# Transposing the larger softmax blocks of seven attention heads by DMA, as half words

## The chip, the cores and the metric

The kernel runs on one core of one Trainium2 chip. The metric is the device time of one execution in microseconds; the time before is the median of three runs. The engines are named as the profile names them: PE is TensorE (PEld its weight loads), DVE is VectorE, ACT is ScalarE, POOL is GpSimd, SP is SyncE, whose queue issues most DMAs.

## The reference

One sequence of 1024 tokens, model width 1024, float32. A recurrent layer (RG-LRU, width 1280), then one attention layer of 8 heads (MLA: keys and values from a 256-wide latent, queries from a 384-wide one, 64 rope dimensions shared by the heads of the key), then a norm. The part that matters here:

```
def one_block(args):                      # one of 8 blocks of 128 queries
    s = einsum("bqhd,bkhd->bhqk", qn_b, k_nope) + einsum("bqhr,bkr->bhqk", qr_b, k_rope)
    s = where(kpos <= qpos, s * ATTN_SCALE, -inf)
    p = softmax(s, axis=-1)
    return einsum("bhqk,bkhd->bqhd", p, v)
...
y = o.reshape(bsz, seq, 8 * 128) * silu(gate)
x = rms_norm(x + y @ w_out, final_norm)
```

## The kernel before, in words

Everything is kept transposed, features on the 128 partitions and tokens along the free axis. Each float32 operand of a product is held as two float32r tiles, a high part and the rest (`hl`: ACT copies the high part, DVE subtracts), and a product is three matmuls: high by high, high by low, low by high (`mm3`). A "page" is a tile of 128 x 1024 words from a pool of 36.

The recurrent layer, the projections of the attention layer and the spills of gates (`gd`), query ropes (`qsd`) and the latent (`kvd`) to HBM take the first 500 us or so. Then comes attention:

- `items` lists 64 items, 8 heads (`hd`) by 8 query blocks (`qb`) of 128 queries. Block `qb` sees `qb + 1` key blocks of 128.
- `scores(hd, qb, ...)` runs two items ahead (`LOOK`). It makes a block of scores in PSUM (tile `s`, two buffers), queries on partitions; DVE adds the mask and takes the maximum, ACT takes the exponential with its sum, DVE the reciprocal and the scaling (L869). The result `p_` is a page.
- `transposes(qb, p_, pts)` turns it, 128 x 128 at a time, on TensorE into PSUM (L877; tile `pm`, four buffers), and `hl` splits the result into the tiles `pt`, high and low, where keys are on partitions.
- `pv(hd, g, pts)` multiplies the values by four query blocks at once (`g` is 0 for blocks 0 to 3, 1 for 4 to 7), one item after the last of them (`PVD`), multiplies by the gate (a page, loaded per head) and splits the result `y`. The split `y` of heads 0 to 5 (`NSPILL`) is spilled to `ysd` by DMAs on POOL's queue.
- `kq` makes the next head's keys and queries and `vals` the values of a pair of heads; their pieces are spread over the items by hand (`KQ_AT`, `V_AT`, `V0_AT`). In the last head `dpart` does part of the output product, from `y` that `yload` has brought back by SP's queue, and `wout` loads the output weights.

The output product, the residual and the norm follow in three chunks of tokens.

The order on each engine is made when the program is built, from priorities in the order of the text and the scheduler's own idea of what is ready; weight loads (`wload`) have their priority raised by 100 instructions (`WPRI`). An engine then runs its instructions in that order, each waiting for its semaphores. DMAs of one queue are issued in order too.

Of the kernel before, what the change touches and what calls it, by code (L numbers as in the profile page):

```python
# [8 lines left out]

F32 = mybir.dt.float32  # L10
F32R = mybir.dt.float32r
AF = mybir.ActivationFunctionType
ALU = mybir.AluOpType
AX = mybir.AxisListType
# [3 lines left out]
S = 1024  # L18
# [3 lines left out]
NH = 8  # L22
# [1 line left out]
SCALE = 192 ** -0.5  # L24
NEG = -1e30
P = 128
NPAGES = 36
NSPILL = 6
WPRI = 100
WOUT_AT = (-1, 1, 2)  # L30
# [13 lines left out]
SPN = (5, 0)  # L44
# [13 lines left out]
def trunk(tc, xT, wina, vecs, wgate, wouta, winc, wuk, wuv, wuq, wuqr, woutb, rope, outT):  # L58
# [15 lines left out]

    def page(dt=F32R):
        return pgs.tile([P, S], dt, tag="pg", name=nm("pg"))

    def f(ap):
        return ap.bitcast(F32)

    def hl(src, hi, lo):
        A.activation(out=hi, in_=src, func=AF.Copy)  # L82
        V.tensor_tensor(out=lo, in0=src, in1=f(hi), op=ALU.subtract)  # L83
# [39 lines left out]
    def hs(h):  # L123
        return slice(h * HW, (h + 1) * HW)
# [44 lines left out]


    pr_ = ExitStack()
    rbp = pr_.enter_context(tc.tile_pool(name="rbp", bufs=1))
    pa = ExitStack()
    ta = pa.enter_context(tc.tile_pool(name="ta", bufs=2))
# [81 lines left out]
    def xsplit(k, c=slice(0, S)):  # L256
        g = vec[:, NA + k:NA + k + 1]
        if len(xs) == k:
            xs.append((page(), page()))
        xh, xl = xs[k][0][:, c], xs[k][1][:, c]  # L260
        A.activation(out=xh, in_=xrs[k][:, c], func=AF.Copy, scale=g)
        V.scalar_tensor_tensor(out=xl, in0=xrs[k][:, c], scalar=g, in1=f(xh), op0=ALU.mult, op1=ALU.subtract)  # L262
# [195 lines left out]

    def fput(i, j, src):
        if fx[i][j // 2] is None:  # L460
            fx[i][j // 2] = (page(), page())
        hi, lo = fx[i][j // 2]
        hl(src, hi[:, hs(j % 2)], lo[:, hs(j % 2)])

# [358 lines left out]
    def vals(pair, half):  # L823

        if half == 0:
            vt[pair] = []
        uh, ul = wload(wuv[pair], 512)
        t = (page(), page())
        vt[pair].append(t)

        def piece(sp):
            ps = pm()
            for sb in range(2):
                o = ps[:, sb * 256:(sb + 1) * 256]
                c0 = (half * 4 + sp * 2 + sb) * P
                for kt in range(2):
                    ch, cl = ckv[kt][0][:, c0:c0 + P], ckv[kt][1][:, c0:c0 + P]
                    u = slice(kt * 256, (kt + 1) * 256)
                    T.matmul(out=o, lhsT=ch, rhs=uh[:, u], start=kt == 0, stop=False)
                    T.matmul(out=o, lhsT=ch, rhs=ul[:, u], start=False, stop=False)  # L840
                    T.matmul(out=o, lhsT=cl, rhs=uh[:, u], start=False, stop=kt == 1)
            hl(ps, t[0][:, hs(sp)], t[1][:, hs(sp)])

        return [lambda sp=sp: piece(sp) for sp in range(2)]

    def scores(hd, qb, k, q, qs):
        nk = (qb + 1) * P
        ps = pss.tile([P, S], F32, tag="s", name=nm("s"))
        ql = slice(qb * P, nk)

        o = P if nk == 5 * P else 0
        sc = ps[:, o:o + nk]
        for c0, c1 in ((0, min(nk, HW - o)), (HW - o, nk)):
            if c0 >= c1:
                continue
            c = slice(c0, c1)
            T.matmul(out=sc[:, c], lhsT=q[0][:, ql], rhs=k[0][:, c], start=True, stop=False)  # L857
            T.matmul(out=sc[:, c], lhsT=q[0][:, ql], rhs=k[1][:, c], start=False, stop=False)  # L858
            T.matmul(out=sc[:, c], lhsT=q[1][:, ql], rhs=k[0][:, c], start=False, stop=False)  # L859
            T.matmul(out=sc[:, c], lhsT=qs[:, ql], rhs=R1[:, c], start=False, stop=False)  # L860
            T.matmul(out=sc[:, c], lhsT=qs[:, ql], rhs=R2[:, c], start=False, stop=True)  # L861
        V.tensor_tensor(out=sc[:, ql], in0=sc[:, ql], in1=mask, op=ALU.add)
        m = tp.tile([P, 1], F32, tag="m", bufs=4, name=nm("m"))
        V.tensor_reduce(out=m, in_=sc, axis=AX.X, op=ALU.max, negate=True)  # L864
        p_ = page(F32)
        l = tp.tile([P, 1], F32, tag="l", bufs=4, name=nm("l"))
        A.activation(out=p_[:, 0:nk], in_=sc, func=AF.Exp, bias=m, accum_out=l)  # L867
        V.reciprocal(out=l, in_=l)
        V.tensor_scalar(out=p_[:, 0:nk], in0=p_[:, 0:nk], scalar1=l, scalar2=None, op0=ALU.mult)  # L869
        return p_  # L870

    def transposes(qb, p_, pts):
        for b0 in range(0, qb + 1, 4):
            b1 = min(qb + 1, b0 + 4)
            ps = pm()
            for b in range(b0, b1):
                T.transpose(out=ps[:, (b - b0) * P:(b - b0 + 1) * P], in_=p_[:, b * P:(b + 1) * P], identity=ident)  # L877
            th, tl = pts[b0 // 4]
            c = (qb % 4) * P
            src = ps[:, 0:(b1 - b0) * P].rearrange("p (k q) -> p k q", q=P)  # L880
            hl(src, th[:, 0:b1 - b0, c:c + P], tl[:, 0:b1 - b0, c:c + P])

    def pv(hd, g, pts):
        ps = pm()
        v = vt[hd // 2]
        nb = 4 * (g + 1)
        for b in range(nb):
            c = slice(max(0, b - 4 * g) * P, HW)
            vs = slice((b % 4) * 256 + (hd % 2) * P, (b % 4) * 256 + (hd % 2) * P + P)
            vh, vl = v[b // 4][0][:, vs], v[b // 4][1][:, vs]  # L890
            th, tl = pts[b // 4][0][:, b % 4, c], pts[b // 4][1][:, b % 4, c]
            T.matmul(out=ps[:, c], lhsT=vh, rhs=th, start=b == 0, stop=False)  # L892
            T.matmul(out=ps[:, c], lhsT=vh, rhs=tl, start=False, stop=False)  # L893
            T.matmul(out=ps[:, c], lhsT=vl, rhs=th, start=False, stop=b == nb - 1)  # L894
        y = gates[hd][:, hs(g)]
        V.tensor_tensor(out=y, in0=ps, in1=y, op=ALU.mult)
# [7 lines left out]
    gates = []  # L904
    ysb = [None] * NH

    ysd = dp.tile([NSPILL, 2, P, S], F32, name="ysd")
# [27 lines left out]
    heads[0], kqwork = kq(0)  # L935
    for wk in kqwork:
        wk()
    kqwork = []
    vwork = vals(0, 0) + vals(0, 1)
    dwork = []  # L940
    ny = 0
    items = [(hd, qb) for hd in range(NH) for qb in range(8)]
    pend = {}
    pts = {}
    late = []
    for i in range(LOOK):
        pend[items[i]] = scores(*items[i], *heads[0])
    for i, (hd, qb) in enumerate(items):
        if qb == 0:
            gt = page(F32)  # L950
            nc.sync.dma_start(out=gt, in_=gd[hd])
            gates.append(gt)
            if hd + 1 < NH:
                heads[hd + 1], kqwork = kq(hd + 1)
        if qb == VQB and hd // 2 + 1 < NH // 2:
            vwork += vals(hd // 2 + 1, hd % 2)
# [6 lines left out]
        if i == 8 * (NH - 1) + DSTART:  # L963
            dwork = [lambda a=a: dpart(*a) for a in DPART]
        for wl, n in ((kqwork, KQ_AT[qb]), (vwork, V0_AT[qb] if hd == 0 and qb < 4 else V_AT[qb]), (dwork, D_AT[qb - DSTART] if i >= 8 * (NH - 1) + DSTART else 0)):
            for _ in range(min(n, len(wl))):
                wl.pop(0)()
        g = qb // 4
        if qb % 4 == 0:
            pts[hd, g] = [tuple(tp.tile([P, 4, HW], F32R, tag=f"pt{i}", name=nm("pt")) for i in range(2)) for _ in range(g + 1)]  # L970
# [3 lines left out]
        if qb % 4 == 3:  # L974
            late.append((i, hd, g, pts.pop((hd, g))))
        j = i - 8 * (NH - 1)
# [137 lines left out]
```

## Time and profile before

| | us |
|---|---|
| median of 3 runs | 875.47 (875.17 to 876.12) |
| the profiled execution, whole | 876.11 |
| its span, first to last instruction | 874.3 |
| busy PE / DVE / ACT / POOL | 857.5 / 659.4 / 517.0 / 75.1 |
| one head of attention (heads 1 to 6) | 31.0 |
| mean granted TensorE clock | 0.994 |

Busy time is the time in which an engine has an instruction in work; matmuls overlap, so the pitch from start to start says what one costs. "A <- B" in the waits means that A's engine sat idle until B ended. In groups of instructions the columns are line, engine, operation, tiles and shapes, count, busy us, mean ns of one, and the idle time before them.

### The profile page before, as it was taken

To read this page: it belongs to the slowest core of one execution; us is meant where nothing else is said; L and a number is where in the kernel's file an instruction comes from. 1 tells how busy PE (TensorE), PEld (TensorE's weight loads), DVE (VectorE), ACT (ScalarE), POOL (GpSimd) and SP (SyncE) were. 2 spreads that over 40 slices of the span, in tenths; PEclk is the share of its full clock that TensorE was granted. 3 is DMA by queue.
4 is the path that set the end of the run, shared out by engine and by line. 5 is a ranking of instruction groups with operands and counts; after the bars stand their busy time and mean duration, and the time that the engine had idled before them with its cause. 6 is when DMAs were issued, how large, how long until landed. Compare 5 with 4: busy or idle time off the path is not lost.

```text
span 874.3 us, 12183 instructions
## 1 busy us (share of the span) xinstructions
PE 857.5 (98%) x4326; PEld 729.6 (83%) x4326; DVE 659.4 (75%) x1224; ACT 517.0 (59%) x956; POOL 75.1 (9%) x145
## 2 busy tenths in 40 slices
PE   8999999999999999999999999999999999999995
PEld 7788888888887888888778888988998998888995
DVE  7798778777877764779988956887797887775453
ACT  7457787777687542699885645555565554431222
POOL 1010110011000100000212320000000000010000
PEclk9999999999999999999999999999999999999998
DMA  8333333333212545133535664222231326666031
GB/s 289 99 97 97 97 96 97 109 101 92 79 37 81 179 132 175 49 108 111 177 122 205 216 229 119 76 82 97 70 112 67 111 67 258 214 216 204 27 126 66
DMA packets 51789, 109.00 MB, mean 125 GB/s; under 512 B 6544, under 2 KB 16656, under 8 KB 51728
## 3 DMA queue, kind: packets, MB, share of 16 engines
q1 hardware_dynamic: 36240, 67.45, 24.2%
q0 software_dynamic: 15216, 40.51, 13.9%
q8 instruction: 34, 0.56, 0.3%
q10 hardware_dynamic: 272, 0.26, 0.1%
q14 instruction: 27, 0.22, 0.1%
HBM read 81.46 MB, written 26.21 MB: 123 GB/s over the span
## 4 chain that ended last, share of the span: by engine, by line
PE 62%; issue 21%; DVE 7%; ACT 4%; DMA 2%; POOL 2%; SPq 0%; DVEq 0%; POOLq 0%; ACTq 0%
PE ps L115 7%; PE ps L116 7%; PE ps L114 7%; PE pm L116 6%; PE pm L115 6%; PE pm L114 6%; PE pm L877 4%; PE pm L894 2%; PE pm L893 2%; PE s L858 2%; PE s L859 2%; PE s L857 2%; PE s L861 2%; PE s L860 2%; PE pm L892 2%
## 5 line engine op out<-in xcount | busy, mean ns | idle before, releaser
L114 PE MATMUL ps<-pg,wh 128*128 128x512 f32 x672 | 262.4, 392 | 3.4 <-DVE tk L627 1.2
L115 PE MATMUL ps<-pg,wh 128*128 128x512 f32 x672 | 262.4, 390 | 0.3 <-DVE pg L262 0.3
L116 PE MATMUL ps<-pg,wl 128*128 128x512 f32 x672 | 262.2, 390 | 0.1
L114 PEld LDWEIGHTS ps<-pg,wh 128*128 128x128 f32 x672 | 126.4, 188 | 31.9 <-DVE tk L627 1.6
L115 PEld LDWEIGHTS ps<-pg,wh 128*128 128x128 f32 x672 | 126.5, 188 | 27.7 <-DVE pg L262 0.6
L116 PEld LDWEIGHTS ps<-pg,wl 128*128 128x128 f32 x672 | 126.6, 188 | 27.1 <-DVE wl L83 1.0
L82 ACT ACTIVATE pt<-pm 128x512 fp32r<-128x512 f32 (+2 forms) x96 | 44.4, 490 | 59.0 <-PE pm L877 55.8
L867 ACT ACTIVATE pg<-s,m 128x128 f32<-128x128 f32 (+3 forms) x64 | 47.5, 743 | 48.0 <-DVE m L864 43.3
L114 PE MATMUL pm<-pg,pg 128*128 128x256 f32 (+1 forms) x192 | 61.9, 322 | 0.0
L115 PE MATMUL pm<-pg,pg 128*128 128x256 f32 (+1 forms) x192 | 61.6, 321 | 0.0
L116 PE MATMUL pm<-pg,pg 128*128 128x256 f32 (+1 forms) x192 | 61.3, 319 | 0.0
L83 DVE TENSOR_TENSOR pt<-pm,pt 128x512 fp32r<-128x512 f32 (+2 forms) x96 | 50.6, 547 | 2.2 <-ACT pt L82 2.1
L864 DVE TENSOR_REDUCE m<-s 128x1 f32<-128x128 f32 (+3 forms) x64 | 48.1, 753 | 1.0
L83 DVE TENSOR_TENSOR wl<-wr,wh 128x512 fp32r<-128x512 f32 (+2 forms) x57 | 32.8, 578 | 17.2 <-ACT wh L82 17.1
L358 DVE SCALAR_TENSOR_TENSOR t<-xb,vec,t 128x512 f32<-128x512 f32 x60 | 44.8, 746 | 0.4
L82 ACT ACTIVATE wh<-wr 128x512 fp32r<-128x512 f32 (+2 forms) x57 | 30.8, 543 | 23.8 <-PE ps L115 9.7
L82 ACT ACTIVATE pg<-pg 128x512 fp32r<-128x512 f32 x42 | 26.2, 630 | 29.9 <-DVE pg L412 18.3
L877 PE MATMUL pm<-ident,pg 128*128 128x128 f32 x288 | 42.3, 274 | 0.3 <-DVE pg L869 0.3
L116 PE MATMUL pm<-pg,wl 128*128 128x512 f32 x108 | 42.3, 392 | 0.0
L115 PE MATMUL pm<-pg,wh 128*128 128x512 f32 x108 | 42.3, 392 | 0.0
L114 PE MATMUL pm<-pg,wh 128*128 128x512 f32 x108 | 42.1, 390 | 0.0
L857 PE MATMUL s<-pg,pg 128*128 128x512 f32 (+2 forms) x96 | 37.2, 388 | 2.0 <-ACT pg L867 2.0
(223 smaller groups left out, 1789.6 us busy)
## 6 DMA issues: line engine op xcount, KB each, us to landing
wr<-wina SPq DMA_DIRECT2D x40, 256.0 KB, 2.8
wh<-wina POOLq DMA_DIRECT2D x36, 256.0 KB, 2.9
wa<-winc SPq DMA_DIRECT2D x24, 256.0 KB, 2.7
ysd<-pg POOLq DMA_DIRECT2D x12, 512.0 KB, 3.2
pg<-ysd SPq DMA_DIRECT2D x12, 512.0 KB, 8.3
wr<-wouta SPq DMA_DIRECT2D x16, 256.0 KB, 2.7
t<-xT SPq DMA_DIRECT2D x16, 256.0 KB, 4.0
x1d<-t POOLq DMA_DIRECT2D x16, 256.0 KB, 3.4
```

Of the source, the lines that this page charges most:

```text
L82: A.activation(out=hi, in_=src, func=AF.Copy)
L83: V.tensor_tensor(out=lo, in0=src, in1=f(hi), op=ALU.subtract)
L114: T.matmul(out=ps, lhsT=w[0], rhs=r[0], start=first, stop=False, skip_group_check=more)
L115: T.matmul(out=ps, lhsT=w[0], rhs=r[1], start=False, stop=False, skip_group_check=more)
L116: T.matmul(out=ps, lhsT=w[1], rhs=r[0], start=False, stop=last, skip_group_check=more)
L358: V.scalar_tensor_tensor(out=xc, in0=xb[:, j:j + HW], scalar=cwv[j], in1=xc, op0=ALU.mult, op1=ALU.add)
L857: T.matmul(out=sc[:, c], lhsT=q[0][:, ql], rhs=k[0][:, c], start=True, stop=False)
L858: T.matmul(out=sc[:, c], lhsT=q[0][:, ql], rhs=k[1][:, c], start=False, stop=False)
L859: T.matmul(out=sc[:, c], lhsT=q[1][:, ql], rhs=k[0][:, c], start=False, stop=False)
L864: V.tensor_reduce(out=m, in_=sc, axis=AX.X, op=ALU.max, negate=True)
L867: A.activation(out=p_[:, 0:nk], in_=sc, func=AF.Exp, bias=m, accum_out=l)
L877: T.transpose(out=ps[:, (b - b0) * P:(b - b0 + 1) * P], in_=p_[:, b * P:(b + 1) * P], identity=ident)
```

## The change

In heads 0 to 6, blocks 5, 6 and 7 (`QD = 5`) are no longer transposed by TensorE. `scores` gives GpSimd a copy of the scaled block as 16-bit halves, all first halves of the words in front and all second halves behind; SP issues one DMA transpose of these 128 x 128 blocks of half words from SBUF to SBUF, back into the page of `p_`; GpSimd joins the halves to words in the copy's page. The split (`psplit`) then reads SBUF instead of PSUM. Such a block is split three items after its turn (`HLAG = 3`), so that blocks 5 to 7 of a head are split at items 0 to 2 of the next, and `pv` of its second half comes at item 3.

With it: the scaling moves from DVE to ACT; the tiles `pt` become one tile for each half and part, without the columns that the causal mask never uses, one buffer each; gates are loaded by halves into a pool of their own; `y` of heads 0 to 5 is spilled unsplit, and `yload` reads it twice, on SP and with a cast on POOL, and DVE subtracts; the pieces of `kq` go to blocks 4 to 6, those of `vals` to even heads; the page pool has 32 pages, and four more are in a pool that ends before attention.

```
-NPAGES = 36
+NPAGES = 32
+NX = 4
-KQ_AT = (1, 0, 1, 0, 2, 0, 0, 0)
-V0_AT = (1, 1, 2, 0)
-V_AT = (0, 0, 0, 0, 0, 0, 1, 1)
+KQB = 2
+KQ_AT = (0, 0, 0, 0, 1, 1, 2, 0)
+V_AT = (0, 0, 1, 1, 0, 1, 1, 0)
+VQB = (1, 4)
+G_AT = (1, 5)
-VQB = 4
+QD = 5
+HLAG = 3
+ROW = 384
...
     (scores)
-        V.tensor_scalar(out=p_[:, 0:nk], in0=p_[:, 0:nk], scalar1=l, scalar2=None, op0=ALU.mult)
-        return p_
+        A.activation(out=p_[:, 0:nk], in_=p_[:, 0:nk], func=AF.Copy, scale=l)
+        if qb < QD or hd == NH - 1:
+            return p_
+        c = pgs.tile([P, 2 * S], U16, tag="pg", name=nm("pu"))
+        p16 = p_.bitcast(U16)
+        G.tensor_copy(out=c[:, 0:2 * nk].rearrange("p (t n) -> p t n", t=2),
+                      in_=p16[:, 0:2 * nk].rearrange("p (n t) -> p t n", t=2))
+        nc.sync.dma_start_transpose(out=p16[:, 0:2 * nk].rearrange("p (b q) -> p b q", q=P), in_=c[:, 0:2 * nk])
+        G.tensor_copy(out=c[:, 0:2 * nk].rearrange("p (n t) -> p t n", t=2),
+                      in_=p16[:, 0:2 * nk].rearrange("p (t n) -> p t n", t=2))
+        return c
...
+    def psplit(qb, c, pt):
+        for b0 in range(0, qb + 1, 4):
+            b1 = min(qb + 1, b0 + 4)
+            bysplit(c.bitcast(F32)[:, b0 * P:b1 * P], qb, b0, b1, pt)
...
     (pv)
-        y = gates[hd][:, hs(g)]
+        y = gates[hd][g]
         V.tensor_tensor(out=y, in0=ps, in1=y, op=ALU.mult)
-        if g == 0:
-            ysb[hd] = (page(), page())
-        hl(y, ysb[hd][0][:, hs(g)], ysb[hd][1][:, hs(g)])
-        if hd < NSPILL and g == 1:
-            for i in range(2):
-                DQ.dma_start(out=ysd[hd, i], in_=f(ysb[hd][i]))
+        if hd < NSPILL:
+            DQ.dma_start(out=ysd[hd, :, hs(g)], in_=y)
+        else:
+            if g == 0:
+                ysb[hd] = (page(), page())
+            hl(y, ysb[hd][0][:, hs(g)], ysb[hd][1][:, hs(g)])
...
     def yload(hd):
-        ysb[hd] = (page(), page())
-        for i in range(2):
-            nc.sync.dma_start(out=f(ysb[hd][i]), in_=ysd[hd, i])
+        hi, lo = ysb[hd] = (page(), page())
+        nc.sync.dma_start(out=f(lo), in_=ysd[hd])
+        G.dma_start(out=hi, in_=ysd[hd])
+        V.tensor_tensor(out=lo, in0=f(lo), in1=f(hi), op=ALU.subtract)
...
+    def block(i, hd, qb):
+        g = qb // 4
+        if qb % 4 == 0:
+            n = (4 * HW if g else 0) + 4 * ROW + P
+            pts[hd, g] = tuple(tp.tile([P, n], F32R, tag=f"pt{g}{a}", bufs=1, name=nm("pt")) for a in range(2))
+        (psplit if qb >= QD and hd < NH - 1 else transposes)(qb, pend.pop((hd, qb)), pts[hd, g])
+        if qb % 4 == 3:
+            late.append((i, hd, g, pts.pop((hd, g))))
...
     for i, (hd, qb) in enumerate(items):
+        if qb == KQB and hd + 1 < NH:
+            heads[hd + 1], kqwork = kq(hd + 1)
+        if hd % 2 == 0 and qb in VQB:
+            vwork += vals(hd // 2, VQB.index(qb))
+        if qb in G_AT:
+            gt = tp.tile([P, HW], F32, tag="gt", bufs=3, name=nm("gt"))
...
         if late and i - late[0][0] >= PVD:
             pv(*late.pop(0)[1:])
-        transposes(qb, pend.pop((hd, qb)), pts[hd, g])
+        while wait and wait[0][0] <= i:
+            block(i, *wait.pop(0)[1:])
+        if qb >= QD and hd < NH - 1:
+            wait.append((i + HLAG, hd, qb))
+        else:
+            block(i, hd, qb)
```

More of the change, by code (lines that the diff above doesn't have):

```diff
@@ L11 @@
 F32R = mybir.dt.float32r
+U16 = mybir.dt.uint16
 AF = mybir.ActivationFunctionType
@@ L258, in xsplit @@
         if len(xs) == k:
-            xs.append((page(), page()))
+            xs.append((page(), page()) if k >= NX // 2 else (xpage(), xpage()))
         xh, xl = xs[k][0][:, c], xs[k][1][:, c]
@@ L868, in scores, with rows, bysplit, transposes @@
         V.reciprocal(out=l, in_=l)
-        V.tensor_scalar(out=p_[:, 0:nk], in0=p_[:, 0:nk], scalar1=l, scalar2=None, op0=ALU.mult)
-        return p_
-    def transposes(qb, p_, pts):
+        A.activation(out=p_[:, 0:nk], in_=p_[:, 0:nk], func=AF.Copy, scale=l)
[9 more added lines that the diff above has]
+        return c
+    def rows(t, qb, b0, b1):
+        o, w, c, b = 0, ROW, (qb % 4) * P, b0
+        if qb >= 4:
+            if b0 < 4:
+                w = HW
+            else:
+                o, b = 4 * HW, b0 - 4
+        d = P if w == ROW and c == ROW else 0
+        return t[:, o + d:o + d + 4 * w].rearrange("p (b s) -> p b s", s=w)[:, b:b + b1 - b0, c - d:c - d + P]
+    def bysplit(src, qb, b0, b1, pt):
+        src = src[:, 0:(b1 - b0) * P].rearrange("p (b q) -> p b q", q=P)
+        hl(src, *(rows(t, qb, b0, b1) for t in pt))
+    def transposes(qb, p_, pt):
         for b0 in range(0, qb + 1, 4):
@@ L937, in trunk @@
         wk()
-    kqwork = []
-    vwork = vals(0, 0) + vals(0, 1)
-    dwork = []
+    kqwork, vwork, dwork = [], [], []
     ny = 0
     items = [(hd, qb) for hd in range(NH) for qb in range(8)]
-    pend = {}
-    pts = {}
+    pend, pts, gates = {}, {}, {}
     late = []
@@ L947, in trunk @@
         pend[items[i]] = scores(*items[i], *heads[0])
-    for i, (hd, qb) in enumerate(items):
[L949 to L956, printed above, removed]
+    def block(i, hd, qb):
[6 more added lines that the diff above has]
+            late.append((i, hd, g, pts.pop((hd, g))))
+    wait = []
+    for i, (hd, qb) in enumerate(items):
+        j = i - 8 * (NH - 1)
+        if qb == KQB and hd + 1 < NH:
[4 more added lines that the diff above has]
+            gt = tp.tile([P, HW], F32, tag="gt", bufs=3, name=nm("gt"))
+            g = G_AT.index(qb)
+            nc.sync.dma_start(out=gt, in_=gd[hd, :, hs(g)])
+            gates.setdefault(hd, []).append(gt)
         if i + LOOK < len(items):
```

32 lines of the change are left out of this document (14 added, 18 removed).

## The prediction

> **What bounds the kernel now.** I read first the busy times and the waits, then the attention stage alone, then the chain in it. Attention (a loop over 64 items, 8 heads by 8 query blocks) runs from about 528 to 784 us.
>
> ```profile
> span 874.3 us, 12183 instructions
> PE 857.5 (98%) x4326; PEld 729.6 (83%) x4326; DVE 659.4 (75%) x1224; ACT 517.0 (59%) x956; POOL 75.1 (9%) x145
> PE s L857 <- ACT pg L867: 2.0, 2, 1.1
> ```
>
> TensorE is busy nearly all the time; its longest wait for anybody totals 2.0 us. The stretches, one per head (columns: span, then busy us and count of PE, PEld, DVE, ACT, POOL, then clock, DMA share, GB/s), say the same of this stage:
>
> ```profile
> 584.60:615.60 31.00, 31.00 (x188) 27.80 (x187) 25.58 (x58) 17.33 (x39) 1.06 (x2) 1.00 0.28 88
> 739.60:784.00 44.40, 43.19 (x243) 36.92 (x242) 34.97 (x73) 17.88 (x41) 3.71 (x7) 1.00 0.67 232
> ```
>
> A head takes 31.0 us and TensorE is busy for 31.0 of them. Whatever leaves its queue comes off the time, and whatever it waits for is added. The chain inside one head shows what the transposes cost it (start, us on the chain):
>
> ```profile
> 553.59 0.57 PE pm L877 x5
> 556.45 0.65 PE pm L877 x6
> 559.10 0.76 PE pm L877 x7
> 561.91 0.87 PE pm L877 x8
> ```
>
> **Transposes removed.** Blocks 5, 6 and 7 of seven heads leave TensorE: 0.65 + 0.76 + 0.87 = 2.28 us a head, 16.0 us in all. Nothing is added to TensorE: the value products read the same columns from another layout, so this term is all gain as long as TensorE never waits.
>
> **The new chain.** Where TensorE used to transpose two items after the scores, a block now goes: scores, softmax, GpSimd copy (halves apart), DMA transpose on SP, GpSimd copy (joined), split by ACT and DVE, then `pv`. The cover is the TensorE work queued between the scores of block 7 and the `pv` that needs it. Its matmuls start at this pitch:
>
> ```profile
> 640.66 0.39 PE L861 MATMUL s<-pg,qs 128*128 128x512 f32 x1
> 640.89 0.34 PE L857 MATMUL s<-pg,pg 128*128 128x384 f32 x1
> 641.07 0.35 PE L858 MATMUL s<-pg,pg 128*128 128x384 f32 x1
> 650.10 0.28 PE L859 MATMUL s<-pg,pg 128*128 128x128 f32 x1
> 650.21 0.27 PE L860 MATMUL s<-pg,qs 128*128 128x128 f32 x1
> 651.08 0.28 PE L841 MATMUL pm<-wh,pg 128*128 128x256 f32 x1
> 651.20 0.29 PE L839 MATMUL pm<-wh,pg 128*128 128x256 f32 x1
> ```
>
> So 0.23 us for 512 columns, 0.18 for 384, 0.11 and 0.12 for 128 and 256. Between lie: a query half (9 x 0.23 = 2.1), both key halves (12 x 0.23 = 2.8), the next head's scores 0 to 5 (0.6, 0.6, 0.9, 1.15, 1.5, 1.75: 6.4 unrounded), the six small transposes of its blocks 0 to 2 (at 0.87/8 = 0.11 each, 0.7), and two pieces of values (2 x 12 x 0.12 = 2.9; two before the head change, or two after it): 14.9 us, the same for even and odd heads.
>
> Against it stands the chain. One softmax of 1024 columns with nothing beside it shows in the last head:
>
> ```profile
> 742.45 0.31 DVE s L862
> 742.78 1.24 DVE m L864
> 744.04 1.21 ACT pg L867 x2
> 745.28 0.16 DVE l L868
> 745.63 0.67 DVE pg L869
> 746.44 1.06 PE pm L877 x8
> ```
>
> That is 3.9 us from 742.45 to 746.3. The scaling moves from DVE to ACT, where 1024 columns SBUF to SBUF take 1139 ns; the split of a first half costs 632 ns there and about as much on DVE:
>
> ```profile
> L261 ACT ACTIVATE pg<-pg,vec 128x1024 fp32r<-128x1024 f32 x7 | 8.0, 1139 | 0.6 <-DMA pg<-xT 0.6
> L83 DVE TENSOR_TENSOR pg<-pg,pg 128x512 fp32r<-128x512 f32 x12 | 8.2, 682 | 0.0
> L82 ACT ACTIVATE pg<-pg 128x512 fp32r<-128x512 f32 x12 | 7.6, 632 | 1.9 <-DVE pg L896 1.5
> ```
>
> Softmax 4.4 us, split 1.3 us: 5.7, to which two copies and a transpose come.
>
> GpSimd copies 2048 half words for block 7 (1536 and 1792 for blocks 5 and 6). No row has such a copy. The nearest:
>
> ```profile
> L1058 POOL TENSOR_TENSOR pg<-pg,acc 128x256 f32<-128x256 f32 x2 | 1.8, 898 | 88.9 <-DVE acc L151 88.9
> masks.py:199 POOL TENSOR_SCALAR_AFFINE_SELECT ident<-ident 128x128 f32<-128x128 f32 x1 | 0.3, 325 | 0.0
> masks.py:197 POOL MEMSET ident<- 128x128 f32 x1 | 0.2, 204 | 0.3 <-POOLq L1106 0.3
> L1106 POOL MEMSET const-float32-0.0<- 128x1 f32 x1 | 0.1, 98 | 0.2 <-issue 0.2
> ```
>
> With 0.1 us fixed, an element costs 0.83 ns written only, 1.77 ns read and written, 3.1 ns with two inputs. A copy reads once and writes once, so it lies between the first two; I take 1.5 ns, 3.2 us for block 7 (bounds 1.8 and 6.5).
>
> The transpose moves 512 KB. The nearest rows move as much or less in plain copies, issued on SP, and the price of an issue there:
>
> ```profile
> pg<-gd SPq DMA_DIRECT2D x8, 512.0 KB, 4.0
> wr<-wuv SPq DMA_DIRECT2D x8, 256.0 KB, 2.7
> pg<-ysd SPq DMA_DIRECT2D x12, 512.0 KB, 8.3
> 554.36 0.33 SPq L91 DMA_DIRECT2D wr<-wuq  x1
> ```
>
> I take 4.0 us, the single load of that size, not the 8.3 of twelve issued in a heap; below, 2.7. [...] No run so far shows a transpose.
>
> Chain: 5.7 + 3.2 + 4.0 + 3.2 = 16.1 us against 14.9: late by 1.2 us, seven times 8.4 us. How much of it TensorE idles depends on its order, which is not the order of the text:
>
> ```profile
> 765.50 0.33 PE L893 MATMUL pm<-pt,pg 128*128 128x384 f32 x1
> 765.67 0.39 PE L114 MATMUL pm<-pg,pg 128*128 128x512 f32 x1
> 765.90 0.34 PE L894 MATMUL pm<-pt,pg 128*128 128x384 f32 x1
> ```
>
> In the last head an output product stands between two matmuls of `pv`: the scheduler fills by readiness. The next scores (2.0 us) and query half (2.1) are there to fill with. I count half of the lateness, 4.2 us.
>
> **Edits costed at nothing.** The scaling on ACT costs 1.0 ns a column, some 5.5 us a head, less two y splits of 0.63: 17.33 + 4.3 = 21.6 of 28.7 us, hidden; DVE gets about 4 us a head lighter by it, and 1.4 by the y splits. The spill of y is halved; the reload's high half goes through GpSimd's queue, and six subtractions of 1024 columns (2 x 0.68 each, 8.2 us) fall on DVE in the last head, which has 44.4 - 35.0 = 9.4 us free and 4 more from the scaling; were that cover gone, up to 8 us. GpSimd gets per head 10,752 elements (16 us at 1.5 ns) and two spill issues: 17 of 28.7 us; the spills queue behind copies, but nothing reads them before the last head. SP's queue stalls behind each transpose's wait for its copy. Queued there: gate halves (needed three and six items later) and weights, which are issued early by priority; the value weights of an even head at block 4 are the tight ones (2.7 + 1.3 us), nothing if the priority puts them ahead of the transposes, 4 x 4.0 us if not. The moves of `kq` and `vals`, the smaller page pool, and half gates change no count of TensorE's work.
>
> **Sum.** The profiled execution took 876.1 us (span 874.3), 0.6 over the median of 875.47. 876.1 - 16.0 + 4.2 = 864.3; against the median, 863.7. I say 864. With all lateness refilled 859.5, with none 868.
>
> **Rivals.**
>
> *DVE comes too late for the splits* (18 in 100). From block 7 to block 2 of the next head TensorE has only 5 to 6 us of work, and DVE nearly 9: four masks (1.2), maxima (2.2 by columns from the 1.24), reciprocals (0.6), the six splits (3.6) and the small ones (1.0). And where DVE and GpSimd both worked on SBUF, at the kernel's end, both had two inputs there:
>
> ```profile
> 866.77 0.43 DVE L151 SCALAR_TENSOR_TENSOR acc<-t,t 128x256 f32<-128x256 f32 x1
> 867.23 3.16 DVE L1058 TENSOR_TENSOR pg<-pg,acc 128x256 f32<-128x256 f32 x6
> 867.34 1.76 POOL L1058 TENSOR_TENSOR pg<-pg,acc 128x256 f32<-128x256 f32 x2 [88.86 <-DVE acc L151]
> ```
>
> Six at 0.43 make 2.6 us, they took 3.16: 0.3 us lost per GpSimd instruction of 0.9 us, some 1 us per copy if it grows with the length. The new splits read two inputs from SBUF, where the old ones read one from PSUM. Against it: the splits are wanted only at `pv`, two or three items on. If it leaves 2.0 us of idle a head in all, 14 us instead of 4.2: 873.5, still faster; from 2.28 us a head on, nothing is gained. [...]
>
> *The transpose is issued in pieces and the change is slower* (17 in 100). If SP issues one piece per 128 x 128 half words, block 7 has 16, at 0.33 us each 5.3 us, and the last lands 2.7 us later: 8.0 us instead of 4.0. The chain is then 20.1 us, late by 5.2, seven times 36 us: 877.7 with half refilled, 896 with none; 887 between. It decides from a transpose of 5.1 us (nothing refilled) to 7.4 us (half). For it speaks that no row shows this instruction; against it that plain copies of the size are one issue.
>
> [...]
>
> *GpSimd becomes the bound* (7 in 100). At the two-input rate of 3.1 ns a head's copies take 33.3 us, with two spill issues 34.4 us against 31: 24 us slower, 899. It decides at 2.8 ns. For it speaks only the row with two inputs.
>
> **How the numbers follow.** My forecast, 859.5 to 868, has 52 in 100; 2 more lie below it (a wait of the last head gone). I call the time the same within 0.2%, 873.7 to 877.2, about what a measurement of this kernel can tell. Faster: 54 and 8 of the DVE rival's 18, 62. Same: 7 of that rival and 1 of the pieces, 8. Slower: 3 of the DVE rival, 16 of the pieces, the small pieces and GpSimd, 30. The range 859 to 890 holds the forecast, the DVE rival and more than half of the pieces; the forecast's own range is 859.5 to 868.
>
> **What would show it.** TensorE has 141 of 288 transposes left. Right: a head of 28.7 to 30 us, with TensorE busy in nearly all of it, its waits at `pv` for DVE's split below 1 us a head; GpSimd copies near 3.2 us and the DMA landing near 4 us for block 7; ACT near 21.6 us a head. Wrong: waits of 2.3 us and more a head ahead of `pv` or of the scores (for ACT's exp, if softmax queues behind the splits); copies well over 3.2 us; a landing over 5 us; DVE instructions with two SBUF inputs well over 0.68 us.

## The result, and the profile after

The change makes the kernel slower: 923.77 us median of 4 runs (922.84 to 925.99) against 875.8 us before on the same chip, ratio 1.0551, 95% interval 1.0527 to 1.0574. The forecast was 864.

The page of the changed kernel, in the order read before: span, busy times, granted clock in tenths over 40 slices, the chain that ended last, and TensorE's three longest waits (us in total, times, longest).

```profile
span 920.9 us, 11981 instructions
PE 869.1 (94%) x4179; PEld 731.2 (79%) x4179; DVE 645.1 (70%) x1154; ACT 553.7 (60%) x1008; POOL 159.4 (17%) x193
...
PEclk9999999999999999999999998998989979799998
...
PE 45%; issue 19%; DMA 12%; ACT 8%; DVE 8%; POOL 8%; SPq 0%; POOLq 0%; DVEq 0%; ACTq 0%
...
PE s L869 <- ACT pg L88: 18.3, 7, 3.7
PE s L869 <- ACT pg L879: 10.7, 9, 2.9
PE s L870 <- DVE pg L89: 3.4, 5, 1.7
```

TensorE has its 147 matmuls fewer, 4179 against 4326. Its idle time went from 874.3 - 857.5 = 16.8 to 920.9 - 869.1 = 51.8 us, 35.0 more; its busy time rose by 11.6 us although 16 us of transposes had gone. So there are two losses: idle, and matmuls that take longer. The idle is not at `pv` (no such row), where the prediction looked for it. It is at `scores`, in the first items of each head: seven times for the split of the next head's keys (L88 of ACT, one for each of seven head changes), nine times for the exponential that frees a score bank, one of the two buffers of the tile `s` (L879).

The stage in windows (as before: span, busy and count by engine, clock, DMA share, GB/s):

```profile
590.00:610.00 20.00, 15.20 (x81) 13.07 (x80) 13.85 (x31) 13.94 (x31) 6.52 (x3) 0.83 0.52 114
610.00:630.00 20.00, 20.00 (x109) 17.48 (x108) 10.58 (x20) 10.26 (x19) 6.09 (x5) 1.00 0.45 93
630.00:650.00 20.00, 15.98 (x75) 13.56 (x75) 14.12 (x32) 13.42 (x32) 6.49 (x3) 0.83 0.41 98
```

The long blocks in the middle of a head (610 to 630) run as they should. Both losses sit at the head changes: TensorE busy for 15.2 of 20 us, at a mean clock of 0.83. From the second head on, heads began every 31.0 us before; now the steps are 33.9 to 39.7 us.

One head change, from 626 us on, engine by engine (start, us, engine, line, operation, and in brackets the idle time before it and what ended it): ACT first, then GpSimd, VectorE and TensorE.

```profile
628.67 1.15 ACT L881 ACTIVATE pg<-pg,l 128x1024 f32<-128x1024 f32 x1
630.12 0.60 ACT L88 ACTIVATE pg<-pm 128x512 fp32r<-128x512 f32 x1
633.24 0.63 ACT L88 ACTIVATE pt<-pu 128x512 fp32r<-128x512 f32 x1 [2.52 <-POOL pu L891]
633.78 0.58 ACT L88 ACTIVATE pg<-pm 128x512 fp32r<-128x512 f32 x1
...
631.04 2.17 POOL L891 COPY pu<-pg 128x1792 uint16<-128x1792 uint16 x1 [5.29 <-DMA pg<-pu]
633.12 1.90 POOL L888 COPY pu<-pg 128x2048 uint16<-128x2048 uint16 x1
639.45 2.52 POOL L891 COPY pu<-pg 128x2048 uint16<-128x2048 uint16 x1 [4.44 <-DMA pg<-pu]
...
633.90 1.66 DVE L89 TENSOR_TENSOR pt<-pu,pt 128x512 fp32r<-128x512 f32 x1 [2.46 <-ACT pt L88]
...
634.41 0.47 PE L869 MATMUL s<-pg,pg 128*128 128x128 f32 x1 [3.72 <-ACT pg L88]
634.68 0.52 PE L853 MATMUL pm<-wh,pg 128*128 128x256 f32 x1
635.00 0.41 PE L851 MATMUL pm<-wh,pg 128*128 128x256 f32 x1
```

ACT stands still for 2.52 us for block 6's joined words (633.24), and the key split that TensorE needs stands right behind it (633.78). TensorE waits 3.72 us for that, and then its matmuls of 256 columns start every 0.21 us, not every 0.12. GpSimd, in order too, holds block 7's first copy back until block 6 is joined: scaled at 629.82 (628.67 + 1.15), copied from 633.12. And VectorE's split of block 6, with both operands in SBUF, takes 1.66 us beside a GpSimd copy, not 0.69.

### The profile page after: what moved, and what is told of

Its sections match the earlier page's. It is cut to its first block, busy times and chain, and to the rows that moved or that the text cites. A ratio compares the mean times of both kernels' runs of the same rounds, so it can differ in the third digit from the quotient of the medians.

```text
span 920.9 us, 11981 instructions
## 1 busy us (share of the span) xinstructions
PE 869.1 (94%) x4179; PEld 731.2 (79%) x4179; DVE 645.1 (70%) x1154; ACT 553.7 (60%) x1008; POOL 159.4 (17%) x193
## 3 DMA queue, kind: packets, MB, share of 16 engines
q1 hardware_dynamic: 74832, 73.94, 28.3%
## 4 chain that ended last, share of the span: by engine, by line
PE 45%; issue 19%; DMA 12%; ACT 8%; DVE 8%; POOL 8%; SPq 0%; POOLq 0%; DVEq 0%; ACTq 0%
PE ps L122 10%; PE ps L121 10%; PE ps L120 9%; DMA pg<-pu 9%; PE pm L121 4%; PE pm L122 4%; PE pm L120 4%; POOL pu L888 4%; POOL pu L891 3%; ACT wa L519 2%; ACT wh L88 1%; DVE wl L89 1%; DVE pg L89 1%; POOL wh L103 1%; DVE t L421 1%
## 5 line engine op out<-in xcount | busy, mean ns | idle before, releaser
L120 PE MATMUL ps<-pg,wh 128*128 128x512 f32 x568 | 220.6, 390 | 2.2 <-DVE tk L639 1.3
L121 PE MATMUL ps<-pg,wh 128*128 128x512 f32 x568 | 221.1, 389 | 0.1
L122 PE MATMUL ps<-pg,wl 128*128 128x512 f32 x568 | 221.0, 389 | 0.1
L120 PEld LDWEIGHTS ps<-pg,wh 128*128 128x128 f32 x568 | 106.4, 188 | 25.6 <-DVE tk L639 1.7
L121 PEld LDWEIGHTS ps<-pg,wh 128*128 128x128 f32 x568 | 106.6, 188 | 22.7 <-DVE pg L89 0.5
L122 PEld LDWEIGHTS ps<-pg,wl 128*128 128x128 f32 x568 | 106.6, 188 | 22.6 <-DVE wl L89 0.6
L879 ACT ACTIVATE pg<-s,m 128x128 f32<-128x128 f32 (+3 forms) x64 | 47.2, 738 | 39.0 <-DVE m L876 30.0
L869 PE MATMUL s<-pg,pg 128*128 128x512 f32 (+2 forms) x96 | 40.7, 429 | 29.1 <-ACT pg L88 18.3
L891 POOL COPY pu<-pg 128x1536 uint16<-128x1536 uint16 (+2 forms) x21 | 46.8, 2228 | 77.5 <-DMA pg<-pu 77.4
L881 ACT ACTIVATE pg<-pg,l 128x128 f32<-128x128 f32 (+3 forms) x64 | 48.9, 773 | 17.8 <-DVE l L880 17.8
L89 DVE TENSOR_TENSOR pt<-pu,pt 128x512 fp32r<-128x512 f32 (+2 forms) x42 | 34.9, 832 | 29.3 <-ACT pt L88 28.6
L888 POOL COPY pu<-pg 128x1536 uint16<-128x1536 uint16 (+2 forms) x21 | 35.3, 1681 | 93.1 <-ACT pg L881 93.1
L103 POOL DMA_DIRECT2D wh<-wina x36 | 19.2, 533 | 181.3 <-PE ps L122 169.3
L869 PEld LDWEIGHTS s<-pg,pg 128*128 128x128 f32 x96 | 20.4, 215 | 37.8 <-ACT pg L88 20.3
L89 DVE TENSOR_TENSOR wl<-wr,wh 128x512 fp32r<-128x512 f32 (+2 forms) x57 | 33.7, 594 | 18.6 <-ACT wh L88 18.5
L88 ACT ACTIVATE pt<-pu 128x512 fp32r<-128x512 f32 (+2 forms) x42 | 23.5, 571 | 34.7 <-POOL pu L891 34.7
L88 ACT ACTIVATE wh<-wr 128x512 fp32r<-128x512 f32 (+2 forms) x57 | 30.5, 539 | 21.1 <-PE ps L121 11.5
```

The source lines that it names most:

```text
L120: T.matmul(out=ps, lhsT=w[0], rhs=r[0], start=first, stop=False, skip_group_check=more)
L121: T.matmul(out=ps, lhsT=w[0], rhs=r[1], start=False, stop=False, skip_group_check=more)
L122: T.matmul(out=ps, lhsT=w[1], rhs=r[0], start=False, stop=last, skip_group_check=more)
L881: A.activation(out=p_[:, 0:nk], in_=p_[:, 0:nk], func=AF.Copy, scale=l)
L888: G.tensor_copy(out=c[:, 0:2 * nk].rearrange("p (t n) -> p t n", t=2), in_=p16[:, 0:2 * nk].rearrange("p (n t) -> p t n", t=2))
L891: G.tensor_copy(out=c[:, 0:2 * nk].rearrange("p (n t) -> p t n", t=2), in_=p16[:, 0:2 * nk].rearrange("p (t n) -> p t n", t=2))
```

## The experiments

Each change is shown against the changed kernel unless it says otherwise; times are medians. The ratios are to the kernel before, run on the same chip (875.5 to 876.3 us).

**Only the DMA path undone** (`pe_all`).

```
-QD = 5
+QD = 8
```

> Only the DMA path is undone (QD = 8: no block is set apart, transposed by DMA or joined); the placement of the projections, the scaling on ScalarE, the new tiles and the y spill stay. If the loss comes from queueing at the head change, in which splits that wait for GpSimd and the DMA stand ahead of the key splits, the waits at scores(hd+1, 0) shrink from 18.3 us to under 8, the granted clock is back above 0.98 and the time is 876 to 890 us. If the placement of the key projection alone is at fault, idle and clock stay as in the changed kernel and the time is 925 to 940 us (16 us of transposes come back). If the scaling on ScalarE is at fault, likewise above 915.

887.38 us, ratio 1.0134 (1.0119 to 1.0149); clock 0.995, and the waits at `scores` for the key split are gone from the list. So the DMA path costs 36.4 us net, and the loss is not the key placement alone. But the other edits, which the prediction had put at nothing, cost 11.6 us by themselves.

**The clock filled by force** (`warm`).

```
+        if qb == 0 and hd:      # ahead of its first matmul
+            for _ in range(12): T.matmul(out=ps[:, HW:], lhsT=R1[:, 0:P], rhs=R1[:, 0:HW], start=True, stop=True)
+        if qb == 1 and hd:      # ahead of the mask: 8 more of the same
```

> The changed kernel with 12 matmuls of 512 columns without use ahead of scores(hd+1, 0) and 8 ahead of the mask of block 1, so that TensorE is busy where it was idle at the head change: 20 x 0.23 = 4.6 us for each of seven heads. If the idle is what halves the clock for some 6 us behind it, the mean granted clock goes from 0.964 to above 0.985 and the 27.6 us of slow clock come back for the most part: 895 to 908 us. If the clock falls for another reason (power, or the stage itself), the clock stays near 0.96 and the time is 921 to 950 us.

953.21 us, 1.0879 (1.0863 to 1.0896), over both expectations; clock 0.969. The dummies delayed the scores behind them, and TensorE then waited for the exponentials (22.9 us in 11 waits, not 10.7 in 9). The idle was moved, not filled (53.5 us in all, not 51.8), so this run tells nothing of the clock.

**The splits put behind the key splits** (`behind`) **and the keys made earlier** (`kq_early`). These tested the first theory, that the key split's place in the queue was the fault.

```
 (behind, in block)
+        if qb > QD and hd < NH - 1:
+            with tc.issue_after(kqlast[0][0]), tc.issue_after(kqlast[0][1]):   # last key split, ACT and DVE
+                psplit(qb, pend.pop((hd, qb)), pts[hd, g])
 (kq_early)
-KQ_AT = (0, 0, 0, 0, 1, 1, 2, 0)
+KQ_AT = (0, 0, 0, 1, 2, 1, 0, 0)
```

> The changed kernel with the splits of blocks 6 and 7 put behind the last key split in the queues of ScalarE and VectorE, and nothing else moved. If the waits at scores(hd+1, 0) come from splits that stand ahead of the key splits and wait for GpSimd's join, PE's wait there falls from 18.3 us for 7 to under 9 and, with the clock, the time to 885 to 905 us. If the DMA and the GpSimd copies are late by themselves, the wait moves to pv and the time stays at 915 to 930 us.

> The changed kernel with the four projections of the next head's queries and keys one to two blocks earlier (done by block 5), so that scores(hd+1, 0) find their keys split long before. If the placement of the key projection makes the idle at the head change, the wait at scores(hd+1, 0) goes, about 18 us of idle and half or more of the slow clock: 880 to 900 us. If the cover of the DMA chain is what is too short, the projections are missing between block 7 and pv and the wait comes back at pv or at the score banks: 915 to 930 us.

929.30 us, 1.0616 (1.0586 to 1.0645), and 941.68 us, 1.0747 (1.0729 to 1.0764). Both theories' numbers were missed by `kq_early`. TensorE's first wait in the one and in the other:

```profile
PE s L871 <- ACT pg L881: 21.8, 13, 3.6
PE s L871 <- ACT pg L88: 12.1, 7, 2.7
```

```profile
PE s L869 <- ACT pg L879: 44.1, 15, 6.7
```

(L881 of the first is L879 of the others, the exponential.) Where the wait for the keys shrinks or goes, the wait for the exponential takes its place and is longer. What is late is ACT itself, and with it whatever stands behind the splits of the DMA blocks. The first theory fell: the keys were only the next in line.

**Splits that wait for nothing** (`free_split`) **and splits one item later** (`hlag4`).

```
 (free_split, in psplit)
-            bysplit(c.bitcast(F32)[:, b0 * P:b1 * P], qb, b0, b1, pt)
+            bysplit(f(R1)[:, b0 * P:b1 * P], qb, b0, b1, pt)
 (hlag4)
-HLAG = 3
+HLAG = 4
```

> The changed kernel with every copy of GpSimd and every DMA transpose still issued, but the splits of blocks 5 to 7 of heads 0 to 6 read a page that has been there since the start of the stage instead of the joined block (so the values behind these blocks are wrong; the work is the same). If the loss is ScalarE and VectorE standing still in their queues for the joined block, with the next head's key splits and softmax behind, it goes: PE's waits at the head change under 8 us in all, clock above 0.985, 862 to 878 us (the 887.4 us without the DMA path less 16.0 us of transposes is 871.4). If GpSimd's copies and the DMA traffic slow the other engines, the time stays above 895 us.

> The changed kernel with the splits of the DMA blocks written one item later (HLAG = 4: block 7's in item (hd+1, 3), pv one item behind). If the chain is only too late for the place where its splits stand in ScalarE's queue, one block more of cover takes most of the wait away: 885 to 905 us. If the next head's short blocks give too little cover (a short item is about 2 us) or pv is then late, the wait moves and the time is 910 to 930 us.

913.61 us, 1.0436 (1.0420 to 1.0451): only 10.2 us of the loss are waits for the joined blocks. And 919.60 us, 1.0501 (1.0479 to 1.0523): a little of those waits, 4 us. In `free_split` a new wait shows where nothing reads the chain; ACT, then TensorE:

```profile
642.28 0.42 ACT L88 ACTIVATE wh<-wr 128x256 fp32r<-128x256 f32 x1 [6.40 <-DMA wr<-wuk]
643.15 0.69 PE L916 MATMUL pm<-ident,pg 128*128 128x128 f32 x2 [5.79 <-DVE wl L89]
```

ACT waited 6.40 us for a weight load. SP issues in order, and its transposes wait for GpSimd's first copy: 120.8 us in 21 waits in this stage of that run. The load stood behind one. So did the reloads of `y` in the last head, five of them issued right behind the last transpose (775.90). TensorE's waits for the two (us in total, times, longest):

```profile
PE pm L120 <- DMA pg<-ysd: 7.7, 1, 7.7
PE pm L916 <- DVE wl L89: 5.8, 1, 5.8
```

In the changed kernel the first is 1.4 us and the second is not there, so the 10.2 us are a net figure: these two waits are 12.1 us longer in `free_split`.

**Splits early or late, chain issued or not** (`no_chain`, `free_here`, `floor`). With the ready page, both can be chosen freely.

```
 (no_chain and floor, in scores)
-        if qb < QD or hd == NH - 1:
+        if True:
             return p_
 (free_here and floor, in the loop over items)
-        if qb >= QD and hd < NH - 1:
-            wait.append((i + HLAG, hd, qb))
-        else:
-            block(i, hd, qb)
+        block(i, hd, qb)
```

> As the run whose splits read a ready page (913.6 us), and GpSimd's copies and the DMA transposes left out as well: no transposes of these blocks at all, the splits still three items late. If the loss comes from where the splits stand (the two splits of a large block, ACT and VectorE, in the short items at the head's start, with TensorE's transposes no longer there as cover), the time stays at 903 to 914 us. If it comes from GpSimd's copies slowing VectorE, or from the DMA traffic, it falls to 864 to 878 us.

> As the run whose splits read a ready page, with all copies of GpSimd and DMA transposes issued, but the splits written in their own item, as the kernel without the DMA path has them, not three items later. If the place of the splits is the cause: 866 to 885 us. If GpSimd and the DMA slow the others: 900 to 914 us.

> Both: splits in their own item from a ready page, no copies of GpSimd, no DMA transposes, and no transposes on TensorE for blocks 5 to 7 of seven heads. It is the most that taking the transposes off TensorE could give with these edits. From the run without the DMA path: 887.4 less 16.0 = 871 us; if the transposes were themselves cover for the softmax of the short blocks, 875 to 890 us.

| us, median | splits in their own item | splits three items late |
|---|---|---|
| no copies, no transposes | 873.45 (`floor`) | 885.59 (`no_chain`) |
| copies and transposes issued, not waited for | 894.67 (`free_here`) | 913.61 (`free_split`) |
| and waited for | | 923.77 (the change) |
| transposed by TensorE | 887.38 (`pe_all`) | |

Ratios to before: 0.9970 (0.9958 to 0.9982), 1.0112 (1.0095 to 1.0128), 1.0218 (1.0186 to 1.0250) for `floor`, `no_chain`, `free_here`. Neither theory alone: moving the splits costs 12.1 us without the chain, the chain's mere presence 21.2 us without the move, and the two together 40.2, which is 6.8 more than their sum. In the profiles `free_split` has 20.7 us more idle time than `no_chain` and 10.0 us more busy time for the same matmuls; 13.5 us of the idle are the two waits for loads shown above, which `no_chain` has not.

**Which part of the chain costs** (`fh_pool`, `fh_dma`, `fh_pool_wl`). From `free_here`: without the transposes; without GpSimd's copies; and the first again, with the weight splits of this stage half on GpSimd.

```
 (fh_pool)
-        nc.sync.dma_start_transpose(...)
 (fh_dma)
-        G.tensor_copy(...)                      # both copies
+        nc.sync.dma_start_transpose(out=c[...], in_=p16[:, 0:2 * nk])
 (fh_pool_wl: fh_pool, and in wload)
+            elif att[0]:                       # true from the start of attention
+                A.activation(out=hi, in_=raw, func=AF.Copy)
+                G.tensor_tensor(out=lo, in0=raw, in1=f(hi), op=ALU.subtract)
```

> As the run with the splits in their own item from a ready page and the chain issued beside them (894.7 us), with the DMA transposes left out: GpSimd's two copies a block alone. If GpSimd's copies stretch VectorE's operations with two operands in SBUF (a weight split of 384 columns took 1.34 us there and 0.55 us without the chain), most of the 21.2 us over the run without the chain (873.5) stay: 887 to 895 us. If the transposes in SyncE's queue, with the weight loads behind them, are the cost: 874 to 880 us.

> The other half: the DMA transposes alone, from the scaled block to a page that nobody reads, without GpSimd's copies. If SyncE's queue and the DMA traffic are the cost: 887 to 895 us. If GpSimd's copies are: 874 to 880 us.

> As the run with GpSimd's copies alone (889.2 us), with the low halves of the weight splits of this stage computed on GpSimd instead of VectorE. In that run the two weight splits a head ran beside block 7's copies and took 1.92 and 1.71 us in place of 0.55 and 0.69: 2.4 us for each of seven heads, 16.7 us, against 15.7 us measured. If that is the mechanism, the time falls to 873 to 879 us. If the copies cost in another way (GpSimd's own delays, SBUF in general), it stays at 885 to 892 us.

889.20 us, 1.0161 (1.0132 to 1.0191); 873.54 us, 0.9973 (0.9960 to 0.9986); 872.33 us, 0.9967 (0.9952 to 0.9981). The transposes alone cost nothing (`floor` is 873.45). The copies alone cost 15.7 us, and the timeline of `fh_pool` says how; VectorE, then GpSimd, around a head change:

```profile
593.33 1.92 DVE L89 TENSOR_TENSOR wl<-wr,wh 128x384 fp32r<-128x384 f32 x1 [0.76 <-ACT wh L88]
595.18 1.27 DVE L89 TENSOR_TENSOR pg<-pm,pg 128x512 fp32r<-128x512 f32 x2
596.38 1.73 DVE L89 TENSOR_TENSOR wl<-wr,wh 128x512 fp32r<-128x512 f32 x1
...
592.95 1.90 POOL L888 COPY pu<-pg 128x2048 uint16<-128x2048 uint16 x1 [1.50 <-ACT pg L881]
594.90 2.71 POOL L890 COPY pu<-pg 128x2048 uint16<-128x2048 uint16 x1
```

The weight split of 384 columns starts at 593.33, while GpSimd copies until 594.85, and ends at 595.25, 0.4 us later; the one of 512 runs into the next copy, until 597.61, and ends at 598.11. Both end 0.4 to 0.5 us after the copy beside them. The split between them (595.18, two at 0.6) has one operand in PSUM and loses nothing. In `floor` the two take 0.55 and 0.69 us; the 2.4 us more, seven times, are 16.8. Taking this stage's weight splits off VectorE brings 16.9 us back, where the copies had cost 15.7. So the copies cost here through the weight splits, whose two operands are in SBUF. What moving these splits gives without any copies was not run; if it gives something by itself, as much of the copies' cost is left for other ways.

Both together cost 5.5 us more than the copies alone (`free_here`), where transposes that wait for copies keep loads waiting in SP's queue: one wait of TensorE for the reload of `y` in the last head is 4.6 us, and `fh_pool` and `floor` have none. That part is read from the waits and was not separated by a run.

**Which other edit costs the 11.6 us** (`pe_all_dve`, `pe_all_kq`, `pe_all_v`, `floor_v`). All with `QD = 8`, except the last, which is `floor`; each puts one edit back as it was before.

```
 (pe_all_dve)
+        V.tensor_scalar(out=p_[:, 0:nk], in0=p_[:, 0:nk], scalar1=l, scalar2=None, op0=ALU.mult)
 (pe_all_kq)
+KQB = 0
+KQ_AT = (1, 0, 1, 0, 2, 0, 0, 0)
 (pe_all_v, floor_v)
+V0_AT = (1, 1, 2, 0)
+V_AT = (0, 0, 0, 0, 0, 0, 1, 1)
...
+        if qb == VQB and hd // 2 + 1 < NH // 2:        # VQB = 4
+            vwork += vals(hd // 2 + 1, hd % 2)
```

> All blocks transposed by TensorE (as in the run without the DMA path, 887.4 us), and the scaling by 1/l back on VectorE. If the 11.5 us that the other edits cost come from ScalarE's queue, lengthened by 1.1 us a large block, the time falls to 876 to 881 us. If they come from where the projections were put, it stays at 885 to 889 us.

> All blocks transposed by TensorE, scaling on ScalarE, and the query and key projections of the next head back where they were (begun at block 0, done by block 4). If the 11.5 us come from keys that are projected just ahead of their scores, 876 to 881 us; if from the scaling on ScalarE, 885 to 889 us.

> All blocks transposed by TensorE, and the value projections back where they were (half of the next pair's in each head, at its last two blocks). Scaling and key placement did not explain the 11.5 us that the other edits cost (887.4); its heads with value work were 34.1 us long and the others 30.5, against 31.0 for each head before. If the value work, all of it in one head of two, is the cause: 875 to 879 us. If it is the single pair of split tiles or the page count: 885 to 889 us.

> The run without any transposes of blocks 5 to 7 of seven heads and with no chain (873.5 us), with the value projections back where they were. If those were the 11.5 us: 859 to 865 us, which is the time that the prediction took for a hidden chain. If not: 871 to 875 us.

887.10 us, 1.0129 (1.0112 to 1.0145); 888.68 us, 1.0146 (1.0129 to 1.0163); 882.33 us, 1.0069 (1.0049 to 1.0089); 870.50 us, 0.9935 (0.9913 to 0.9957). Scaling and keys are not it. The values are 5.1 us of it (3.0 on `floor`), less than expected; some 6.5 us stay open, among the one pair of split tiles, the smaller page pool, the half gates and the new spill and reload of `y`.

**What helped, put into the changed kernel** (`after_wl`: the weight splits half on GpSimd; `best`: that, the values as before and `HLAG = 4`).

> The changed kernel with that one edit (low halves of this stage's weight splits on GpSimd). If the stretched weight splits are a third of the loss in the real kernel too, 905 to 913 us; if its waits for the joined blocks swallow it, or the chain grows by GpSimd's added work (some 1 to 2 us a head), 918 to 928 us.

> All that helped, in one kernel that computes the reference: DMA chain kept, weight splits' low halves on GpSimd, value projections back where they were, splits one item later. The single gains add up to 16 + 4 + 4 us: some 900 us, range 888 to 915. It would have to reach 875 to beat the kernel before, which is not expected.

928.03 us, 1.0602 (1.0586 to 1.0618), and 922.66 us, 1.0541 (1.0523 to 1.0560): nothing gained, and the second misses its range. The gains of the runs without waits do not add up here. VectorE's groups in the changed kernel (count, busy, mean ns, idle before) show why the first found nothing to take away:

```profile
L89 DVE TENSOR_TENSOR pt<-pu,pt 128x512 fp32r<-128x512 f32 x22 | 20.0, 908 | 22.0 <-ACT pt L88 21.8
L89 DVE TENSOR_TENSOR wl<-wr,wh 128x512 fp32r<-128x512 f32 x6 | 4.1, 677 | 0.0
L89 DVE TENSOR_TENSOR wl<-wr,wh 128x384 fp32r<-128x384 f32 x5 | 2.8, 559 | 2.3 <-ACT wh L88 2.3
```

With real waits the schedule slips, and GpSimd's copies meet the splits of the DMA blocks (908 ns, not the 684 of `fh_pool`), not the weight splits (677 and 559). In `after_wl` it is the last, short splits of the DMA blocks (384 columns: 1783 ns, not the 548 of `fh_pool`). Which instruction meets the copies hangs on how the schedule falls. No version with the whole computation beat the kernel before. The ceiling with these edits, were the chain to cost nothing, is `floor_v`: 5.2 us or 0.65% below before. What the idea could give without the 6.5 us that stay open was not run.

## Why the prediction was wrong, step by step

| step | put at | shown |
|---|---|---|
| transposes off TensorE | -16.0 | -13.9 (`floor` against `pe_all`) |
| chain late at `pv`, half refilled | +4.2 | no wait at `pv`; +10.2 in waits of ACT's and VectorE's queues |
| splits three items late | 0 | +12.1 (`no_chain` against `floor`) |
| copies and transposes beside the others | 0 | +28.0 with late splits, +21.2 without |
| the other edits | 0 | +11.6 (`pe_all`) |

From 875.8 these make 923.8, as they must: each is the difference of two runs in a row. The order in which the steps are taken moves 6.8 us between the third and the fourth.

*The transposes* were right in kind and 2.1 us too large. From `pe_all` to `floor` TensorE's busy time falls by 18.6 us (865.4 to 846.8), but its idle time rises by 4.7 (19.7 to 24.4): its waits for the exponential grow from 2.0 to 5.7 us, and one of 2.0 us for the key split is new. "All gain as long as TensorE never waits" had that condition, and it did not hold, even without a chain.

*The chain's parts* were shorter than taken. GpSimd's copies of block 7, and the transposes (count, median us to landing):

```profile
L891 POOL COPY pu<-pg 128x2048 uint16<-128x2048 uint16 x6 | 15.1, 2509 | 27.7 <-DMA pg<-pu 27.7
L888 POOL COPY pu<-pg 128x2048 uint16<-128x2048 uint16 x6 | 11.4, 1895 | 2.6 <-ACT pg L881 2.6
pg<-pu SPq DMA_TRANSPOSE x21, 4.3
```

1.9 + 4.3 + 2.5 = 8.7 us where 10.4 were taken; with 5.7 for softmax and split 14.4 us, under the cover of 14.9. But the chain as it ran was longer than its parts. From the end of the scaling to the joined words block 7 took 8.9 us in the first head and 9.9 to 12.2 in the other six, because GpSimd was still joining block 6 and the first copy started 1.1 to 3.3 us late. The sum has no term for that queue. With 5.7 the chain is 14.6 to 17.9 us: that its length came out near the 16.1 of the prediction is luck, two errors against each other.

The rivals in which the transpose comes in pieces, or GpSimd is the bound, fell: one issue that takes SP 1.3 to 2.1 us and lands in 4.3, and GpSimd's six copies take 11.7 us a head. The small pieces that the chances count under slower no run shows: the 21 blocks were 21 issues. The 4.0 us taken for the transpose, from the plain load of 512 KB in the kernel before (`pg<-gd`), was 0.3 us short of the 4.3 in which the transposes landed in the median.

*The step that failed* is the place of the wait: "wait at `pv`", and with it, in the DVE rival, "the splits are wanted only at `pv`". Nobody on TensorE wants them sooner, but ACT and VectorE run in order (at 633.24 ACT had stood 2.52 us, with a key split behind), and the next head's key splits, masks and exponentials are queued behind them. TensorE, short of work in the short items, then waits for those: 32.4 us at `scores` in the changed kernel (18.3 + 10.7 + 3.4), 2.0 us before, and none at `pv`. Later splits alone, with nothing to wait for, cost 12.1 us that the prediction put at nothing. The list of what would show it wrong had the right sign (waits ahead of the scores, for ACT's exponential), and that rival the right mechanism; but it was priced at 2.0 us of idle a head and ended faster than before.

*Edits costed at nothing* failed as a step: "change no count of TensorE's work" was true (4326 matmuls with `QD = 8`) and beside the point.

*VectorE beside GpSimd* was priced as 0.3 us for each GpSimd instruction of 0.9 us, some 1 us a copy. In `fh_pool` it was about the rest of the copy's length: 1.37 us on a 384-column split that began 1.52 us before the copy's end.

*The clock* was in no step. The changed kernel and `floor` give TensorE the same 4179 matmuls; against `floor` (span 871.2, busy 846.8) the changed kernel has 27.4 us more idle and 22.3 us more busy time, mean clock 0.964 against 0.993. The matmuls around gaps, in the changed kernel and in `fh_pool`:

```profile
560.93 0.33 PE L869 MATMUL s<-pg,pg 128*128 128x128 f32 x1 [1.58 <-ACT pg L88]
561.09 0.34 PE L853 MATMUL pm<-wh,pg 128*128 128x256 f32 x1
561.26 0.28 PE L869 MATMUL s<-pg,pg 128*128 128x256 f32 x1
563.19 0.48 PE L870 MATMUL s<-pg,pg 128*128 128x128 f32 x1 [1.65 <-DVE pg L89]
563.47 0.42 PE L871 MATMUL s<-pg,pg 128*128 128x128 f32 x1
563.68 0.41 PE L872 MATMUL s<-pg,qs 128*128 128x128 f32 x1
```

```profile
599.19 0.44 PE L869 MATMUL s<-pg,pg 128*128 128x384 f32 x1 [1.15 <-ACT pg L879]
599.47 0.34 PE L870 MATMUL s<-pg,pg 128*128 128x384 f32 x1
599.64 0.34 PE L871 MATMUL s<-pg,pg 128*128 128x384 f32 x1
599.82 0.34 PE L872 MATMUL s<-pg,qs 128*128 128x384 f32 x1
```

After a first gap of 1.58 us three matmuls come at a granted clock of 1.00 (560.93 to 561.54); in the next gap, of 1.65 us, it falls, and behind that gap 128 columns start every 0.21 us, not every 0.11, and the granted clock is 0.50 until 568.5. After 1.15 us in `fh_pool` 384 columns start every 0.17 to 0.18, as before. In the changed kernel every head change has gaps of 1.6 to 3.7 us and one stretch at half pitch and a granted clock of 0.50, which begins at a gap or up to 1.2 us behind it and lasts from 3.4 to 10.2 us, later gaps included; one gap alone does not decide it (behind one of 2.35 us, at 668.90, ten matmuls come at full pitch). In `fh_pool` twelve gaps of 0.99 to 1.24 us between 564 and 728 us are followed by no such stretch, and its clock is 0.993. Yet at the start of attention, in the changed kernel, one of 0.99 us (531.20) is followed by 3.4 us at 0.50.

What a gap costs beside its length differs. With the same 4179 matmuls, `fh_pool` has 12.4 us more idle time than `floor` and 2.9 more busy time, `free_split` 28.3 and 14.1, `kq_early` 47.2 and 21.8, the changed kernel 27.4 and 22.3. The cause is inferred from this pairing in the traces; the run meant to prove it (`warm`) did not. How much idle time brings a slow stretch on, and what ends it, no run shows.

## What to carry to other kernels

Before a consumer is moved later or made to wait, list what stands behind it in the queues of its own in-order engines; the engine that reads its result last is not the one to ask. A path of helpers can be priced in parts before it is believed: issue it with nobody reading it, let its readers read something ready, and leave it out, in all combinations. Idle time on TensorE at a stage change can cost more than its length: in these runs each us of it came with 0.2 to 0.8 us of slower matmuls.

## What the runs showed of the hardware

- A VectorE subtraction with both operands in SBUF, begun while GpSimd copies within SBUF, ended only after the copy did: 1.92 us in `fh_pool` where `floor` has 0.55. One with an operand in PSUM, beside the next copy, took its usual 0.6.
- GpSimd copied half words at 0.9 ns each when it set them apart (1.90 us for 2048 in the changed kernel) and 1.2 ns when it joined them (2.51 us).
- An SBUF to SBUF DMA transpose of 384 to 512 KB of half words was one issue, took SP 1.3 to 2.1 us to issue where a plain load takes mostly 0.3 to 0.4, landed in 4.3 us (median of 21), and beside the rest of the kernel cost nothing measurable (873.54 us in `fh_dma` against 873.45 in `floor`). What did cost was its place in SP's queue while it waited: loads behind it kept TensorE waiting for 5.8 and 7.7 us in `free_split`.
- Two gaps of 1.6 us on TensorE, near one another, were followed by a granted clock of 0.50 for over 5 us (changed kernel, the second up to 563.19); twelve gaps of 0.99 to 1.24 us in `fh_pool` were not. One of 0.99 us at the start of attention in the changed kernel was, for 3.4 us.
